# A two-layer encoder trunk on one core: the FFN's norm factor moved behind gate and up, one set of weight pools for all stages, and the last hidden pair kept on chip

## Chip, core and metric

One core of a Trainium2 chip runs one program. The metric is its device time in microseconds (us), the median of the runs shown. TensorE (PE) multiplies; VectorE (DVE), ScalarE (ACT) and GpSimd (POOL) work elementwise; SyncE (SP) issues every DMA of this program, in order.

## What is computed

A residual stream h of 1024 tokens by 1024 features goes through two layers in float32. Layer 0 mixes tokens with differential attention, layer 1 with neighbourhood attention. Cut to what matters here:

```
for i in range(DEPTH):                                    # DEPTH = 2
    h = h + mixer_i(rmsnorm(h, norm_mix[i]))              # attention, then @ w_o
    h = h + swiglu(rmsnorm(h, norm_ffn[i]), w_gate, w_up, w_down)
    gate = sigmoid(rmsnorm(h, norm_ple[i]) @ ple_w_gate[i])
    h = h + gate * (p[i] @ ple_w_proj[i])
return rmsnorm(h, norm_final)

def rmsnorm(x, g):  return x * rsqrt(mean(x*x) + eps) * g
def swiglu(h, wg, wu, wd):  return (silu(h @ wg) * (h @ wu)) @ wd    # hidden width 2816
```

## The kernel before

Activations lie feature-major: a tile holds 128 features by 1024 tokens (two halves of 512). Every float32 operand is split into a high and a low part (`split`, L99: ACT or POOL writes the high part, DVE subtracts it from the source for the low part), and a product is three matmul passes, high by high, high by low and low by high (`PASSES`).

The stages of a layer, in the order of the program:

- **Mixer**, `diff_attention` (L300) or `neighborhood_attention` (L438), with `qk` (L231) and `v_units` (L287) for its projections, both by L219 or L294 on the normed input `hnT`. Eight pairs of heads leave split outputs `ot`; seven go to DRAM (`keep`, L548), the last stays on chip. `out_proj_first` (L554) multiplies the first `EARLY = 6` pairs by w_o, adds the residual and stores the sum in DRAM (`hp`); its matmuls (L572) fill the gaps of the last attention unit.
- **Out projection**, `out_proj` (L578): the remaining two pairs (L597), added to `hp` (L599); per half of the tokens `norm_blocks` (L147) then computes the norm (`norm`, L114: ACT squares, DVE sums them, PE sums over partitions at L126, a POOL power, DVE writes diagonals at L132, PE broadcasts them at L134, and DVE multiplies each of the 8 feature tiles at L137).
- **Gate and up**, `gate_up` (L604): both matrices are multiplied by a 2x2 block scheme with seven products instead of eight (`seven`, L209; order 0, 5, 4, 1, 6, 3, 2). Its moving operands are seven tiles `bt` (16 KB a partition each), sums and differences of the four blocks of the normed activations that `norm_blocks` makes with DVE and POOL. Its stationary operands are seven such sums of the weights: `prepare` loads two raw tiles, `blocks` (L180) makes four sums on POOL (L190) and splits seven results on ACT and DVE. There are 11 pairs of 256 hidden features, a group for gate and a group for up in each, and a group is 7 products of 12 matmuls (84) into four PSUM banks. `after` (L641) adds the products, applies silu (L637) or multiplies by the gate (L639). `hand_over` (L664) makes seven blocks of the pair's result (POOL L673, then `split`) and writes them to DRAM (`ad`, L671).
- **Down**, `down` (L693): five chunks of pairs (2, 2, 2, 2, 3); per chunk the blocks `b` come back from DRAM (L706, a ring of 22 tiles), and four output pairs `dp` of seven products each run at L719, with weights through `blocks` again. DVE and POOL add into h at L725; h itself is loaded from DRAM (`hd`, L821).
- **Input embedding**, `ple` (L747): p @ w_proj at L762 from operands loaded before `down`, a norm, 16 blocks of the gate product (L219), then the next norm.

Buffers come from pools on a stack, and a new tile's first write waits for the last reader of what lay at that place. `stage` (raw weights), `slab` (split weights) and `t4` (work tiles) are opened and closed with the stages (`pools`, L86; `build`, L785). What an engine does in which order is set by a scheduler that walks a modelled timeline, so it isn't the order of the code; each engine, SP included, then takes its own list strictly in order.

Of the kernel before, what the change touches and what calls it, by code (L numbers as in the profile page):

```python
# [12 lines left out]
F32 = mybir.dt.float32  # L13
# [18 lines left out]
CHUNKS = ((0, 1), (2, 3), (4, 5), (6, 7), (8, 9, 10))  # L32

# [15 lines left out]
EARLY = 6  # L49
# [5 lines left out]
class Trunk:  # L55
    def __init__(self, ctx, tc, a):
# [5 lines left out]
        self.stage = self.slab = self.t4 = self.ob = None  # L62
# [5 lines left out]
        self.mhalf = self.const.tile([P, 4], F32, name="mhalf")  # L68
# [17 lines left out]
    def pools(self, st, name, **bufs):  # L86
        for k, n in bufs.items():
            setattr(self, k, st.enter_context(self.tc.tile_pool(name=f"{k}_{name}", bufs=n, reuse_waits="tile")))
# [25 lines left out]
    def norm(self, h, c, i, pool, sink, order=range(KT), keep=None):  # L114
# [20 lines left out]
        for k in order:  # L135
            n = keep[:, k] if keep is not None else pool.tile([P, HALF], F32, tag="n", name="n", bufs=4)
# [10 lines left out]
    def norm_blocks(self, h, half, i, pool, bt):  # L147
        nc = self.nc
        c = slice(half * HALF, (half + 1) * HALF)

        def put(b, k, x):
            self.split((bt[b][:, 0, k], bt[b][:, 1, k]), x, nc.scalar)

        if half == 0:
            self.n0 = pool.tile([P, KT, HALF], F32, tag="n0", name="n0", bufs=1)
            self.norm(h, c, i, pool, lambda k, n: put(k // 4, k % 4, n), keep=self.n0)
            return
        n0, held = self.n0, {}

        def sink(k, n):  # L160
            if k < 4:
                held[k] = n
                return
            k -= 4
            n11, n21, n12, n22 = n0[:, k], n0[:, k + 4], held.pop(k), n
            put(2, k, n22)
            nc.gpsimd.tensor_tensor(out=n11, in0=n12, in1=n11, op=ALU.subtract)
            put(4, k, n11)
            nc.gpsimd.tensor_tensor(out=n12, in0=n22, in1=n12, op=ALU.subtract)
            put(6, k, n12)  # L170
            t2 = pool.tile([P, HALF], F32, tag="t2", name="t2", bufs=2)
            nc.vector.tensor_tensor(out=t2, in0=n22, in1=n11, op=ALU.subtract)
            put(5, k, t2)
            nc.gpsimd.tensor_tensor(out=n21, in0=n21, in1=t2, op=ALU.subtract)
            put(3, k, n21)

        self.norm(h, c, i, pool, sink, order=(0, 4, 1, 5, 2, 6, 3, 7))


    def blocks(self, a11, a12, a21, a22, pool, tag, shape, bufs):  # L180
        nc = self.nc
        out = [None] * 7

        def put(b, x):
            w = pool.tile([P, 2] + shape, F32R, tag=tag, name="w", bufs=bufs)
            self.split((w[:, 0], w[:, 1]), x, nc.scalar)
            out[b] = w

        def sub(o, x, y, op=ALU.subtract):
            nc.gpsimd.tensor_tensor(out=o, in0=x, in1=y, op=op)  # L190

        put(0, a11)
        s1 = pool.tile([P] + shape, F32, tag="s1", name="s1", bufs=1)
        s2 = pool.tile([P] + shape, F32, tag="s2", name="s2", bufs=1)
# [36 lines left out]
    def qk(self, u, pools, bias=None, q_scale=1.0):  # L231
        nc = self.nc
        qkp, psd = pools["qk"], pools["d"]
# [4 lines left out]
        for which in range(2):  # L238
            w = self.weights(pools["wqk"][2 * u + which], self.slab, "slab")
            b = None if bias is None else bias[:, which * 8 + u:which * 8 + u + 1]  # L240
            for half in range(2):
# [27 lines left out]
                else:  # L269
# [4 lines left out]
                    for x in (kh, kl):  # L274
                        for m, (to, src) in enumerate(((bot, top), (top, bot))):
                            nc.gpsimd.tensor_scalar(out=x[to, m, c], in0=x[src, m, c].bitcast(F32), scalar1=1.0,
                                                    scalar2=0.0, op0=ALU.mult, op1=ALU.add)
        return qs, kh, kl
# [8 lines left out]
    def v_units(self, pair2, wv, psd, sink, ws=None):  # L287
        ws = ws or [self.weights(wv[2 * pair2 + s], self.slab, "slab") for s in range(2)]
        for t in range(NT):
            ps = psd.tile([P, 256], F32, tag="d", name="d")  # L290
# [9 lines left out]
    def diff_attention(self, first):  # L300
        nc, tc, a = self.nc, self.tc, self.a
        with ExitStack() as st:
            pool = lambda name, bufs, **k: st.enter_context(tc.tile_pool(name=name, bufs=bufs, reuse_waits="tile", **k))
            pools = {"qk": pool("da_qk", 1), "wqk": a["da_qk"]}
            vp = pool("da_v", 1)
# [132 lines left out]
    def neighborhood_attention(self):  # L438
        nc, tc, a = self.nc, self.tc, self.a
        with ExitStack() as st:  # L440
            pool = lambda name, bufs, **k: st.enter_context(tc.tile_pool(name=name, bufs=bufs, reuse_waits="tile", **k))
            pools = {"qk": pool("na_qk", 1), "wqk": a["na_qk"]}
            vp = pool("na_v", 1)
# [11 lines left out]
            def values(p4, psd):  # L455
# [8 lines left out]
                self.v_units(p4, a["na_v"], psd, sink)  # L464
# [72 lines left out]
            values(0, psd)  # L537
            ops = self.qk(0, pools, bq)
# [39 lines left out]
    def out_proj(self, layer, wo, h, ps, np, op, bt):  # L578
# [8 lines left out]
        ws = []  # L587
        for dt in range(KT):
            ws.append(self.weights(wo[dt, :, EARLY * P:], op, f"w{dt}", cols=late * P))
            nc.sync.dma_start(out=h[dt], in_=self.hp[dt])  # L590
        for half in range(2):
            c = slice(half * HALF, (half + 1) * HALF)
            for dt in range(KT):
                acc = ps.tile([P, HALF], F32, tag="mm", name="mm")
                for k in range(late):
                    for n, (i, j) in enumerate(PASSES):
# [313 lines left out]
```

## Time and profile before

| | us |
|---|---|
| median of 3 runs | 3023.63 (3020.64 to 3026.23) |
| the profiled execution | 3023.98 |
| its span, first to last instruction | 3022.2 |
| PE busy | 2739.8 (91%) |
| DVE, POOL, ACT busy | 2130.2, 1325.6, 1217.8 |
| mean granted TensorE clock | 0.956 |

The page of the profile gives busy shares and 40 slices of the span. Idle time of PE is best read from its list of waits and from its timeline, and the load of the other engines from a table by stage, since a share over the whole span mixes stages with different limits.

### The profile page before, as it was taken

Reading aid. Unit: us, or ns where it says so; the run is one execution under the profiler, and the core shown is the slowest. Engines: PE = TensorE matmul, PEld = TensorE weight load, DVE = VectorE, ACT = ScalarE, POOL = GpSimd, SP = SyncE. Lnnn points to the kernel's source line nnn. Section 1 sums busy time; section 2 is a strip of 40 time slices with the busy share of each in tenths; the row PEclk is TensorE's granted clock in tenths of the full one; section 3 lists DMA queues with packets and bytes.
Section 4 is the critical chain, followed back from the end, with each engine's and each line's share of the span. In section 5 each row is a group of like instructions: output and inputs, shape, how many; then the busy total and the mean of one; then the engine's idle time right before and its main releaser. Section 6 shows DMA issues by size and latency. Waiting matters only on the chain. (4 is left out here: it accounts for less than half of the span.)

```text
span 3022.2 us, 38402 instructions
## 1 busy us (share of the span) xinstructions
PE 2739.8 (91%) x13272; PEld 2255.1 (75%) x13272; DVE 2130.2 (70%) x3947; ACT 1217.8 (40%) x2534; POOL 1325.6 (44%) x1240
## 2 busy tenths in 40 slices
PE   6999999997599999599997999999399999789998
PEld 5787888885477878478786888888287788567876
DVE  6798878776767666498584666765866667568766
ACT  4454546443444443233332544542344344323241
POOL 1344443431555555477221443432255555457621
PEclk8999999998799999799998999999699999989999
DMA  3001010324244443866132112144333444486312
GB/s 114 28 29 42 29 42 27 147 100 160 63 153 141 145 154 133 313 258 251 35 119 82 54 69 75 47 170 163 117 116 143 153 153 153 159 330 252 138 63 105
DMA packets 106321, 379.59 MB, mean 126 GB/s; under 512 B 12176, under 2 KB 14352, under 8 KB 102032
## 3 DMA queue, kind: packets, MB, share of 16 engines
q1 hardware_dynamic: 106128, 377.15, 34.5%
q8 instruction: 105, 1.72, 0.2%
q14 instruction: 88, 0.72, 0.1%
HBM read 256.52 MB, written 120.59 MB: 125 GB/s over the span
## 5 line engine op out<-in xcount | busy, mean ns | idle before, releaser
L631 PE MATMUL mm<-bt,w 128*128 128x512 f32 x3696 | 870.4, 397 | 62.6 <-ACT w L101 59.6
L631 PEld LDWEIGHTS mm<-bt,w 128*128 128x128 f32 x3696 | 695.2, 189 | 240.2 <-ACT w L101 62.7
L719 PE MATMUL mm<-b,w 128*128 128x512 f32 x1848 | 432.8, 395 | 72.0 <-DMA b<-ad 63.2
L719 PEld LDWEIGHTS mm<-b,w 128*128 128x128 f32 x1848 | 348.1, 190 | 156.8 <-issue 65.2
L104 DVE TENSOR_TENSOR w<-raw,w 128x512 fp32r<-128x512 f32 (+2 forms) x420 | 356.2, 865 | 50.8 <-ACT w L101 50.4
L219 PE MATMUL d<-hnT,w 128*128 128x512 f32 x1536 | 386.3, 399 | 0.0
L219 PEld LDWEIGHTS d<-hnT,w 128*128 128x128 f32 x1536 | 287.0, 189 | 64.3
L101 ACT CAST w<-raw 128x512 fp32r<-128x512 f32 (+2 forms) x420 | 210.6, 527 | 213.0 <-POOL raw L190 109.2
L103 POOL TENSOR_SCALAR w<-st 128x1024 fp32r<-128x1024 f32 (+2 forms) x120 | 134.3, 1121 | 335.5 <-PE mm L219 100.9
L294 PE MATMUL d<-w,hnT 128*128 128x256 f32 x1536 | 227.2, 294 | 16.0 <-POOL w L103 7.7
L294 PEld LDWEIGHTS d<-w,hnT 128*128 128x128 f32 x1536 | 210.5, 198 | 27.7 <-POOL w L103 9.3
L725 POOL TENSOR_TENSOR h<-h,u 128x512 f32<-128x512 f32 x120 | 169.4, 1426 | 119.0 <-DVE u L725 118.4
L104 DVE TENSOR_TENSOR w<-s,w 128x512 fp32r<-128x512 f32 (+2 forms) x168 | 123.4, 749 | 126.4 <-ACT w L101 126.4
L190 POOL TENSOR_TENSOR s<-raw 128x512 f32<-128x512 f32 (+2 forms) x84 | 95.3, 1134 | 267.2 <-DMA raw<-gu 221.0
L366 ACT ACTIVATE e<-e,mx 128x1024 f32<-128x1024 f32 x128 | 147.3, 1151 | 124.7 <-DVE mx L364 113.4
L104 DVE TENSOR_TENSOR w<-st,w 128x1024 fp32r<-128x1024 f32 (+2 forms) x120 | 136.7, 1141 | 82.4 <-POOL w L103 81.4
L219 PE MATMUL mm<-hnT,w 128*128 128x512 f32 x768 | 188.5, 406 | 4.8 <-ACT hnT L101 3.2
L219 PEld LDWEIGHTS mm<-hnT,w 128*128 128x128 f32 x768 | 147.1, 193 | 45.4 <-issue 7.4
L101 ACT CAST at<-tr 128x512 fp32r<-128x512 f32 (+2 forms) x288 | 132.0, 481 | 106.2 <-PE tr L515 67.5
L281 PE MATMUL s<-kh,qs 128*128 128x512 f32 (+2 forms) x384 | 153.4, 409 | 23.2 <-DVE mx L358 12.6
L104 DVE TENSOR_TENSOR at<-tr,at 128x512 fp32r<-128x512 f32 (+2 forms) x288 | 155.7, 550 | 22.5 <-ACT at L101 16.7
L381 POOL TENSOR_SCALAR e<-e,rc 128x1024 f32<-128x1024 f32 x64 | 74.2, 1160 | 217.3 <-DVE rc L379 212.1
(144 smaller groups left out, 4608.1 us busy)
## 6 DMA issues: line engine op xcount, KB each, us to landing
ad<-put SPq DMA_DIRECT2D x154, 512.0 KB, 2.8
b<-ad SPq DMA_DIRECT2D x154, 512.0 KB, 8.4
raw<-gu SPq DMA_DIRECT2D x88, 512.0 KB, 4.8
raw<-wd SPq DMA_DIRECT2D x32, 512.0 KB, 7.3
st<-wpg SPq DMA_DIRECT2D x32, 512.0 KB, 3.6
ot<-ot SPq DMA_DIRECT2D x14, 1024.0 KB, 3.9
o<-ot SPq DMA_DIRECT2D x14, 1024.0 KB, 7.9
st<-da_qk SPq DMA_DIRECT2D x16, 512.0 KB, 3.4
```

Of the source, the lines that this page charges most:

```text
L101: hi_engine.copy(out=w[0], in_=src)
L103: hi_engine.tensor_scalar(out=w[0], in0=src, scalar1=1.0, scalar2=0.0, op0=ALU.mult, op1=ALU.add)
L104: self.nc.vector.tensor_tensor(out=w[1], in0=src, in1=w[0].bitcast(F32), op=ALU.subtract)
L190: nc.gpsimd.tensor_tensor(out=o, in0=x, in1=y, op=op)
L219: self.nc.tensor.matmul(ps, w[:, i, kt * P:(kt + 1) * P], self.hnT[half][:, j, kt, :], start=kt == 0 and n == 0, stop=kt == KT - 1 and n == 2)
L281: self.nc.tensor.matmul(s, qs[:, m, qc], (kh, kl)[part][:, m, kc], start=part == 0, stop=part == 1)
L294: self.nc.tensor.matmul(ps, self.hnT[t // 4][:, i, k, c], ws[k // 4][:, j, (k % 4) * 256:(k % 4 + 1) * 256], start=k == 0 and n == 0, stop ...
L366: nc.scalar.activation(out=e[m], in_=e[m], func=AF.Exp, bias=mx[:, m:m + 1], scale=SLOPES[h], accum_out=sm[:, m:m + 1])
L381: nc.gpsimd.tensor_scalar(out=e[0], in0=e[0], scalar1=rc[:, 0:1], scalar2=0.0, op0=ALU.mult, op1=ALU.add)
L631: nc.tensor.matmul(acc, w[b][:, i, k * P:(k + 1) * P], bt[b][:, j, k], start=first and k == 0 and n == 0, stop=k == 3 and n == 2, skip_gro ...
L719: nc.tensor.matmul(acc, w[b][:, i, q], mv[b, q][:, j], start=first and q == 0 and m == 0, stop=q == n - 1 and m == 2, skip_group_check=True)
L725: eng.tensor_tensor(out=o, in0=x, in1=y, op=ALU.add)
```

## The change

- **Norm.** `norm_blocks` goes. `out_proj` takes tiles dt and dt + 4 together, multiplies x by the norm's gain alone (ACT), makes the seven `bt` of these two tiles at once (`moving_blocks`) and collects squares (ACT into one `sq` buffer, POOL adds). The factor 1/rms is computed once for all 1024 tokens (`inverse_rms`), issued inside the first gate group after product 5, and kept as `rb`. In `use` the gate's product is multiplied by `rb` before silu, and by `rb` again after it, which brings up's factor.
- **Pools.** One `stage` (2), `slab` (3) and `t4` (4) live as long as the kernel. `packed` puts the seven weight results into slabs (2 to a slab in gate and up, 4 in a two-pair chunk of down) over three shared slabs and two of the stage's own.
- **Down.** The last pair's seven blocks stay on chip (`kept`); the ring has 18 tiles, and the loads of the first chunk and `kept` lie where `bt` was. A three-pair weight tile comes as two loads.
- **Input embedding.** Its operands are loaded and split after `down` (`ple_proj`), through the ring's tiles.
- **Smaller.** `EARLY` is 5, so the late out projection has 3 pairs. Layer 1 computes the first half of its values and half of its first q before it needs the second half of the normed tokens (`lead`). Pools of odd and even head units stand apart.

```diff
-EARLY = 6
+EARLY = 5
+RING_B = 18
...
+        self.pools(ctx, stage=2, slab=3, t4=4)
...
+    def moving_blocks(self, n, k, pool, bt):
...
+        put(0, n11)
+        sub(t3, n22, n12, nc.gpsimd)
+        sub(n12, n12, n11)
+        sub(t2, n22, n12)
+        put(5, t2)
+        put(4, n12)
+        put(1, n21)
+        put(6, t3)
+        sub(n21, n21, t2, nc.gpsimd)
+        put(3, n21)
+        put(2, n22)
+    def inverse_rms(self, acc, diag, rb):
...
+        for b in range(NT):
+            nc.tensor.matmul(ps[:, 0, b:b + 1], acc[:, b * P:(b + 1) * P], self.mean, start=True, stop=True)
...
+        nc.gpsimd.tensor_tensor(out=rs, in0=rs, in1=self.mhalf, op=ALU.pow)
+        for half in range(2):
+            for b in range(4):
+                nc.vector.tensor_scalar(out=diag[:, half, b], in0=self.ident, scalar1=rs[:, 4 * half + b:4 * half + b + 1],
+                                        scalar2=None, op0=ALU.mult)
+            bc = self.ps_tr.tile([P, 4, P], F32, tag="tr", name="bc")
+            nc.tensor.matmul(bc, self.ones1, diag[:, half], start=True, stop=True)
+            nc.scalar.copy(out=rb[:, half * HALF:(half + 1) * HALF], in_=bc.rearrange("p a b -> p (a b)"))
+    def packed(self, slabs):
+        state = [None, 0, 0]
+        def place(n):
+            if state[0] is None or state[1] + 2 * n > 2 * D:
+                pool, tag = slabs[state[2] % len(slabs)]
+                state[:] = [pool.tile([P, 2 * D], F32R, tag=tag, name="w"), 0, state[2] + 1]
...
     def out_proj
+        for k in range(KT // 2):
+            for dt in (k, k + KT // 2):
+                w = self.weights(wo[dt, :, EARLY * P:], op, "w", cols=late * P, bufs=2)
...
+                    nc.vector.tensor_tensor(out=x[:, c], in0=ac, in1=x[:, c], op=ALU.add)
+                    nc.scalar.activation(out=g[:, c], in_=x[:, c], func=AF.Copy,
+                                         scale=self.g[:, 3 * layer + 1, dt:dt + 1])
+                nc.sync.dma_start(out=self.hd[dt], in_=x)
+            self.moving_blocks(n, k, op, bt)
...
+                    sq = op.tile([P, HALF], F32, tag="sq", name="sq", bufs=1)
+                    nc.scalar.activation(out=sq, in_=x[:, c], func=AF.Square)
+                    nc.gpsimd.tensor_tensor(out=acc[:, c], in0=acc[:, c], in1=sq, op=ALU.add)
...
     def gate_up
                 def use(f, c, src, eng):
                     if which == 0:
-                        nc.scalar.activation(out=gt[:, f, c], in_=src, func=AF.Silu)
+                        eng.tensor_tensor(out=o, in0=src, in1=rb[:, c], op=ALU.mult)
+                        nc.scalar.activation(out=o, in_=o, func=AF.Silu)
+                        nc.gpsimd.tensor_tensor(out=o, in0=o, in1=rb[:, c], op=ALU.mult)
...
                     elif b == 5:
-                        add(out=t["u2"], in0=acc, in1=t["p1"], op=ALU.add)
+                        add(out=t["u2"], in0=ac, in1=t["p1"], op=ALU.add)
+                        if pr == 0 and which == 0:
+                            with tc.issue_after(self.end.ins):
+                                self.inverse_rms(acc, op, rb)
...
+            bp.release()
+            bp = tc.alloc_tile_pool(name=f"db{layer}", bufs=1, side="right", reuse_waits="tile")
+            ring = [self.ring_load(bp, pr, b) for b in ORDER for pr in CHUNKS[0]]
+            kept = {b: bp.tile([P, 2, HALF], F32R, tag=f"k{b}", name="kept") for b in range(7)}
+            hand_over(PAIRS_F - 1, kept.get)
...
     def build
-                    pt = [self.weights(a["pT"][layer, k], pw, f"pt{k}") for k in range(2)]
-                    wpp = [self.weights(a["wpp"][layer, k], pw, f"wp{k}") for k in range(2)]
-                    self.down(layer, h, ps)
+                self.down(layer, h, ps, bp, ring, kept)
+                proj = self.ple_proj(layer, ps, bp, pool("pj"))
```

The order of instructions moves at three places that the prediction speaks of.

SP's list at the start of layer 0's `down`, before (`b` are the blocks that `down` reads back, `put` those that `hand_over` writes, `raw` weights, `h` the residual stream):

```order
L821 DMA h_10849<-hd 128x1024
L710 DMA raw<-wd 128x1024
L671 DMA ad<-put 128x1024
L710 DMA raw<-wd 128x1024
L671 DMA ad<-put 128x1024 x3
L710 DMA raw<-wd 128x1024
L108 DMA st<-pT 128x1024
L706 DMA b<-ad 128x1024 x12
L108 DMA st<-pT 128x1024
L706 DMA b<-ad 128x1024 x9
```

The same place now:

```order
L754 DMA ad<-put 128x1024 x6
L810 DMA raw<-wd 128x1024 x3
L787 DMA b<-ad 128x1024 x18
L937 DMA h_10797<-hd 128x1024
L937 DMA h_10798<-hd 128x1024
L937 DMA h_10799<-hd 128x1024
```

The eight loads of h stood ahead of the blocks and now stand behind 18 of them; three weight loads stand ahead of both. The same rows with the semaphores that they wait for:

```order
L810 DMA raw_10978<-wd 128x1024 [waits DMAHW3_49,DMAHW1_49,DVE_49]
L787 DMA b_10735<-ad_95 128x1024 [waits DMAHW4_49,PE_49]
L787 DMA b_10737<-ad_95 128x1024 [waits DMAHW5_49,PE_49]
L787 DMA b_10739<-ad_95 128x1024 [waits DMAHW6_49]
L787 DMA b_10741<-ad_95 128x1024 [waits DMAHW7_49]
```

Only the first two loads of blocks wait for PE. By the semaphore's values in the built program the first waits for product 0 of the last group and the second for product 3, the sixth of seven (it lies where `bt` 3 was), and the third weight load waits for the DVE split that frees the first one's stage buffer; the rest stand behind them.

PE's list where layer 0 goes from the out projection into gate and up, before (`bt` numbers: 7088 is block 0, 7093 block 5, 7092 block 4):

```order
L597 MATMUL mm<-o,w 128x512 x3
L597 MATMUL mm<-ot,w 128x512 x3
L126 MATMUL sums<-mean,acc 128x1 x4
L134 MATMUL bc<-diag,ones_73 128x512
L126 MATMUL sums<-mean,acc 128x1 x4
L134 MATMUL bc<-diag,ones_73 128x512
L631 MATMUL mm<-bt_7088,w 128x512 x12
```

Now (7039 is block 0, 7040 block 5, 7042 block 1, 7043 block 6, 7044 block 3, 7045 block 2):

```order
L707 MATMUL mm<-bt_7042,w 128x512 x2
L707 MATMUL mm<-bt_7044,w 128x512 x6
L179 MATMUL sums<-mean,acc 128x1 x4
L707 MATMUL mm<-bt_7043,w 128x512 x12
L179 MATMUL sums<-mean,acc 128x1 x4
L188 MATMUL bc<-diag,ones_82 128x512 x2
L707 MATMUL mm<-bt_7045,w 128x512 x12
L707 MATMUL mm<-bt_7039,w 128x512 x12
L707 MATMUL mm<-bt_7042,w 128x512 x12
L707 MATMUL mm<-bt_7040,w 128x512 x2
```

Both sums and both broadcasts stood between the out projection and the first product; now one pair of broadcasts stands late in the first group.

PE's list from layer 0's last gate block to layer 1's first values, before:

```order
L219 MATMUL mm<-hnT_12897,w 128x512 x120
L126 MATMUL sums<-mean,acc 128x1 x4
L134 MATMUL bc<-diag,ones_73 128x512
L294 MATMUL d<-w,hnT_12896 128x256 x96
L294 MATMUL d<-w,hnT_12897 128x256 x96
```

Now (`hnT_12899` is the first half of the tokens, `hnT_12900` the second):

```order
L261 MATMUL mm<-hnT_12900,w 128x512 x122
L348 MATMUL d<-w,hnT_12899 128x256 x48
L128 MATMUL sums<-mean,acc 128x1 x4
L348 MATMUL d<-w,hnT_12899 128x256 x39
L136 MATMUL bc<-diag,ones_82 128x512
L348 MATMUL d<-w,hnT_12899 128x256 x9
L261 MATMUL d<-hnT_12899,w 128x512 x24
L348 MATMUL d<-w,hnT_12900 128x256 x96
```

The norm of the second half stood alone ahead of layer 1's values; now 96 value matmuls and 24 of q stand around it.

## Rows read from the trace of the kernel before

**Rows 1.** The page: busy time by engine, the 40 slices of PE and its granted clock.

```profile
PE 2739.8 (91%) x13272; PEld 2255.1 (75%) x13272; DVE 2130.2 (70%) x3947; ACT 1217.8 (40%) x2534; POOL 1325.6 (44%) x1240
...
PE   6999999997599999599997999999399999789998
...
PEclk8999999998799999799998999999699999989999
```

**Rows 2.** Waits of PE, longest first: us in total, times, longest.

```profile
PE mm L719 <- DMA b<-ad: 63.2, 14, 29.7
PE mm L631 <- ACT w L101: 59.6, 2, 29.8
PE sums L126 <- DVE acc L123: 48.1, 5, 14.4
```

**Rows 3.** Table by stage: stretch, length, busy us (instructions), clock, DMA share, GB/s.

```profile
756.00:786.00 30.00, 0.42 (x1) 0.42 (x2) 30.00 (x31) 12.53 (x21) 18.57 (x12) 0.50 0.11 35
786.00:1222.00 436.00, 434.70 (x1848) 347.16 (x1847) 290.38 (x347) 177.75 (x315) 230.79 (x161) 0.99 0.40 137
1222.00:1252.00 30.00, 0.47 (x1) 0.50 (x2) 12.61 (x20) 6.44 (x16) 15.08 (x16) 0.54 0.89 335
```

**Rows 4.** Table by stage again, over two entries into gate and up and one into down.

```profile
711.10:828.10 117.00, 66.00 (x268) 51.38 (x269) 88.49 (x121) 46.40 (x78) 45.01 (x32) 0.77 0.30 104
1222.00:1276.80 54.80, 22.98 (x85) 16.38 (x86) 26.71 (x41) 11.06 (x27) 23.66 (x24) 0.72 0.95 369
2106.30:2231.00 124.70, 75.32 (x311) 59.22 (x310) 88.66 (x121) 46.46 (x78) 43.97 (x31) 0.78 0.33 115
```

**Rows 5.** Timeline of layer 0's entry: start, us, engine, line, tiles, count, idle before.

```profile
711.10 0.42 DVE L104 TENSOR_TENSOR ot<-o,ot 128x256 fp32r<-128x256 f32 x1 [0.47 <-ACT ot L101]
...
741.73 4.29 DVE L104 TENSOR_TENSOR bt<-n,bt 128x512 fp32r<-128x512 f32 x7
...
749.57 1.83 PE L126 MATMUL sums<-mean,acc 128*128 128x1 f32 x8 [14.37 <-DVE acc L123]
...
753.75 2.04 PE L134 MATMUL bc<-diag,ones 128*128 128x512 f32 x2 [2.34 <-DVE diag L132]
```

**Rows 6.** Groups by line and shape in gate and up, 830 to 1200: busy, mean ns.

```profile
L673 POOL TENSOR_TENSOR t<-gt 128x512 f32<-128x512 f32 x20 | 33.5, 1675 | 24.9 <-DVE gt L639 24.9
L190 POOL TENSOR_TENSOR s<-s,raw 128x512 f32<-128x512 f32 x18 | 23.3, 1295 | 0.7
L104 DVE TENSOR_TENSOR put<-gt,put 128x512 fp32r<-128x512 f32 x49 | 54.6, 1129 | 1.1
L646 DVE TENSOR_TENSOR u<-mm,p 128x512 f32<-128x512 f32 x19 | 12.9, 680 | 0.0
```

**Rows 7.** Timeline of DVE and POOL in gate and up, 1030 to 1040.

```profile
1030.31 2.38 DVE L104 TENSOR_TENSOR put<-gt,put 128x512 fp32r<-128x512 f32 x2
1030.53 1.61 POOL L673 TENSOR_TENSOR t<-gt 128x512 f32<-128x512 f32 x1 [2.49 <-DVE gt L639]
...
1037.93 1.62 POOL L673 TENSOR_TENSOR gt<-gt,t 128x512 f32<-128x512 f32 x1
1038.54 1.56 DVE L104 TENSOR_TENSOR put<-t,put 128x512 fp32r<-128x512 f32 x1
```

**Rows 8.** Timeline of SP at the entry into down: blocks read back.

```profile
1257.80 10.56 SPq L706 DMA_DIRECT2D b<-ad  x9
```

**Rows 9.** Loads of the embedding's gate weights: time to landing.

```profile
DMA to landing us min/median/max: 3.3/3.6/5.2
```

**Rows 10.** Timeline of PE at the end of layer 0.

```profile
1589.80 8.33 PE L219 MATMUL mm<-hnT,w 128*128 128x512 f32 x35
1602.48 1.21 PE L126 MATMUL sums<-mean,acc 128*128 128x1 f32 x8 [4.36 <-DVE acc L123]
...
1616.63 0.79 PE L294 MATMUL d<-w,hnT 128*128 128x256 f32 x2 [7.73 <-POOL w L103]
1620.30 5.90 PE L294 MATMUL d<-w,hnT 128*128 128x256 f32 x35 [2.87 <-DVE w L104]
```

More of the change, by code (lines that the diff above doesn't have):

```diff
@@ L134, in norm @@
         nc.tensor.matmul(bc[:, :nb], self.ones1, diag[:, :nb], start=True, stop=True)
-        for k in order:
-            n = keep[:, k] if keep is not None else pool.tile([P, HALF], F32, tag="n", name="n", bufs=4)
+        for k in range(KT):
+            n = pool.tile([P, HALF], F32, tag="n", name="n", bufs=4)
             nc.vector.scalar_tensor_tensor(out=n[:, :w], in0=h(k, c), scalar=self.g[:, i, k:k + 1],
@@ L144, in norm_t, with put @@
         self.norm(h, c, i, pool, lambda k, n: self.split((dst[:, 0, k, o], dst[:, 1, k, o]), n, self.nc.scalar))
[L147 removed]
+    def moving_blocks(self, n, k, pool, bt):
         nc = self.nc
[L149 to L151 removed]
+        n11, n12, n21, n22 = n[0][:, :HALF], n[0][:, HALF:], n[1][:, :HALF], n[1][:, HALF:]
+        def put(b, x):
             self.split((bt[b][:, 0, k], bt[b][:, 1, k]), x, nc.scalar)
[L154 to L177, printed above, removed]
@@ L192, in blocks, with sub @@
+        def sub(os, xs, ys, op=ALU.subtract):
+            for o, x, y in zip(os, xs, ys):
+                nc.gpsimd.tensor_tensor(out=o, in0=x, in1=y, op=op)
+        a11, a12, a21, a22 = zip(*parts)
+        s1, s2, o = [], [], 0
+        for x, n in zip(a11, widths):
+            for j, l in enumerate((s1, s2)):
+                v = sums[:, j, o:o + n]
+                l.append(v.rearrange("p (q c) -> p q c", c=x.shape[2]) if len(x.shape) == 3 else v)
+            o += n
         put(0, a11)
-        s1 = pool.tile([P] + shape, F32, tag="s1", name="s1", bufs=1)
@@ L586, in out_proj @@
         os.append(self.last.rearrange("p l b q -> p l (b q)"))
[L587 to L596, printed above, removed]
-                        nc.tensor.matmul(acc, ws[dt][:, i, k * P:(k + 1) * P], os[k][:, j, c],
-                                         start=k == 0 and n == 0, stop=k == late - 1 and n == 2)
-                nc.vector.tensor_tensor(out=h[dt][:, c], in0=acc, in1=h[dt][:, c], op=ALU.add)
-                nc.sync.dma_start(out=self.hd[dt, :, c], in_=h[dt][:, c])
-            self.norm_blocks(lambda k, c: h[k][:, c], half, 3 * layer + 1, np, bt)
+        acc = op.tile([P, S], F32, tag="acc", name="acc")
@@ L785, in build @@
+                if not last:
+                    nc.sync.dma_start(out=self.hs[dt, :, c], in_=h[dt][:, c])
+            if last:
+                self.norm(hv, c, 3 * layer + 3, np,
+                          lambda k, n: nc.sync.dma_start(out=a["out"][k, :, c], in_=n))
+            else:
+                self.norm_t(hv, c, 3 * layer + 3, np)
     def build(self):
@@ new lines, in build @@
+                if layer == 0:
+                    first = []
+                    with tc.tile_pool(name="x", bufs=1, reuse_waits="tile") as xp:
+                        for q in range(4):
+                            xt = xp.tile([P, KT, 256], F32, tag="x", name="xt", bufs=4)
+                            nc.sync.dma_start(out=xt, in_=a["xq"][q])
+                            if q in (1, 2):
+                                first.append(self.weights(a["da_v"][q - 1], self.slab, "slab"))
+                            self.norm_t(lambda k, c, xt=xt: xt[:, k], slice(q * 256, (q + 1) * 256), 0, xp)
+                    self.diff_attention(first)
+                else:
+                    self.neighborhood_attention()
```

314 lines of the change are left out of this document (185 added, 129 removed).

## The prediction

> **What bounds the kernel now.** I read the page first, then PE's waits, the tables by stage, and the timeline of the places with low busy shares. The page shows PE busy for 91% of the span, with dips in the slices and a lower granted clock in the same slices [rows 1]. So PE is the bound where it runs, and what can be won lies in the dips: 3022.2 less 2739.8 is 282 us. PE's waits name them: the two longest are the entries into gate and up (L631 waits for a weight split, 29.8 us at most, and L126 for the norm's sum, 14.4), and the entries into down (L719 waits for blocks, 29.7) [rows 2]. The tables by stage show what limits each. In the first entry DVE is busy for all of 30 us and POOL for 18.57, PE for 0.42. Gate and up proper is PE alone: 434.70 of 436 us, or 434.70 / 1848 = 0.235 us a matmul, DVE at 290.38. In the down entry the DMA engines are full (0.89) [rows 3]. These two sorts of entry cost 117.0, 124.7 and, for down's first, 54.8 us [rows 4].
>
> Two durations carry most of the sum. A DVE split with both inputs in SBUF takes 4.29 / 7 = 0.61 us where POOL is idle [rows 5]. A POOL tensor_tensor on 512 columns takes 1.295 us in the weight sums, 1.675 in hand_over; the DVE splits beside it go up to 1.129, while L646, which reads PSUM, stays at 0.680 [rows 6]. So DVE operations on SBUF and POOL's stretch each other. How much: in 756 to 786, the 31 DVE instructions are 24 with two SBUF inputs and 7 that read PSUM, and 24 x 0.61 + 12 x 1.29 = 30.1 of 30.00 us: nothing overlapped [rows 3]. In 1030.31 to 1040.10, five POOL operations (5 x 1.29) and seven such DVE operations (7 x 0.61) are 10.7 us of work in 9.79, a ratio of 0.91 [rows 7]. These are my two bounds for work that the change adds there.
>
> The sum is made against the profiled execution, 3023.98; the median is 3023.63, the same but for 0.35.
>
> **A, the entry into gate and up.** Removed: the norm ahead of the blocks, with its wait of 14.37 for the last sum, then 2.34, and the 29.8 after it [rows 2, 5]. In their place the out projection makes the blocks tile by tile and PE multiplies as they come. By the order of the changed kernel, from the split that ends the attention to the last block DVE has 48 operations on SBUF (48 x 0.61 = 29.3) and POOL 28 (22 by 1.29 = 28.4, and six weight roundings of 384 columns at half that, an estimate, 3.9). Taken one after another, as in 756 to 786, that is 61.6, and 4.4 until the first product is there: 66. Then POOL still has four additions of squares (5.2) before the sums, the power, diagonals and broadcast (1.83 + 2.34 + 2.04 as before, 6.2 [rows 5]): 77.4. PE's remaining 36 matmuls of the first group (8.4), a wait of some 3 for a weight of the second group, since POOL multiplies by `rb` before it makes that weight's sums, and 60 of the second group (14.1) give 102.9 until the end of the second group. `EARLY = 5` puts 48 matmuls (11.3 us) into this stretch, where PE waits anyway; out of layer 0's tail it takes 33, worth 0 to 33 x 0.235 = 7.8, taken at half, 3.9. So layer 0 gains 117.0 + 3.9 - 102.9 = 18.0 and layer 1 124.7 - 102.9 = 21.8 [rows 4]: **-40**. Ends: at a ratio of 0.91 the 61.6 become 56, -51; if layer 0's and 1's first blocks come late by the waits for `t4` buffers that x now shares with the weight sums, 10 in each, -20.
>
> **B, the entry into down.** Counted from the start of up's last group (19.7 us of PE, 84 x 0.235), PE has work until 19.7. SP's list decides: the third weight load waits for a split at about 16, the second load of blocks for product 3 (72 matmuls, 16.9), the other 16 behind it. One load of 512 KB follows another every (10.56 - 0.32) / 8 = 1.28 us in such a burst [rows 8]; the first lands some 3.6 after it is issued, by the loads that stand alone [rows 9]. So block 12 lands at 19.8 + 12 x 1.28 = 35.2, block 18 at 42.8 and the first of h at 44.1. The DVE addition with h frees the PSUM bank that the second output pair wants: PE goes on at about 44.9, with the 42 matmuls of the first pair and two more (44, 10.3 us) done meanwhile, a loss of 44.9 - 19.7 - 10.3 = 15, and 3 for additions piled up. Before it was 54.8, of which 85 matmuls are 85 x 0.235 = 20.0: a loss of 35 [rows 4]. **-17 in each layer, -34.** Ends: with blocks landing before product 3 is over, -40; with h at the end of a slower queue and PE waiting all the way, as now, -6.
>
> **C, layer 0 to layer 1.** PE waits 4.36, does the sums, and waits on to 7.73 and 2.87: from 1589.80 + 8.33 = 1598.1 to 1620.3 are 22.2 us with little in them [rows 10]. Now 96 half-width value matmuls and 24 of q need only the first half, and cover it: 96 x 5.90 / 35 = 16.2 [rows 10] and 24 x 0.235 = 5.6. Left is a first weight's split, so **-17**, between -21 and -8.
>
> **D, gate and up.** Added per pair: 8 multiplications by `rb`, five on POOL and three on DVE, one of those from PSUM. POOL has 20 operations of 1.29 a pair instead of 15, DVE 25 on two SBUF inputs. One after another that is 25.8 + 25 x 0.61 = 41.1, against PE's 168 x 0.235 = 39.5 a pair: +1.6 in each of 22 pairs, +35. By the ratio 0.91 it is 37.4 and hidden behind PE: 0. The longer stretch of alternation speaks for the second, the exclusive 30 us for the first, and I take the middle: **+18**.
>
> The Trainium skill, "SBUF — State Buffer", section on the two separate sides, says that DVE and GpSimd share a port pair under a lock held for a whole instruction, the loser blocked; it speaks against putting more POOL work here. The trace agrees in that L646, which reads PSUM, keeps its 0.680 us [rows 6], and differs in the 0.91 [rows 7]. By the rule D would be +35 and the total 2970.
>
> **E, smaller.** The embedding's operands are now loaded and split after down: 8 loads and 8 splits, of which the first can stand on the path (3.6 to land [rows 9], half of it covered): **+2**, 0 to 6. The weight loads of a three-pair chunk are twice as many, of half the size, on an engine that has room in 786 to 1222 (DMA share 0.40 [rows 3]): 0, the cover being the 63 matmuls, 14.8 us, that PE does with each of these tiles. The `kept` pair saves seven stores and loads of 512 KB a layer; they were beside other work outside the entry: 0.
>
> Sum: -40 - 34 - 17 + 18 + 2 = -71, so 3024 - 71 = **2953 us**.
>
> **Rivals.** (1) Gate and up stays with PE and the entries come out at their good ends: -51 - 40 - 20 + 0 + 0 = -111, 2913; from 2895 on. The ratio in rows 7 speaks for it, the full DVE of rows 3 against. (2) Down's entry gains nothing, since SP takes its list in order and h stands behind 18 blocks: the stall by blocks becomes a stall by h. Then B is 0 and the sum -37, 2987, up to 3010 with D at 35. For it speaks that the DMA engines are full there already (0.89 [rows 3]); against, that seven blocks of the last pair don't travel. (3) The side that is slower: gate and up becomes DVE's. DVE must do, per pair, 25 operations on SBUF and 10 from PSUM (10 x 0.68 = 6.8); it exceeds PE's 39.5 when an SBUF operation takes over 32.7 / 25 = 1.31 on average. Splits are now at 1.129 beside POOL [rows 6]; POOL's busy share there goes from 230.79 / 436 = 0.53 [rows 3] by 20 / 15 to 0.71. The stretch over 0.61 being 0.52 at a share of 0.53, it is 0.70 at 0.71: 1.31, just at the point. At 1.56, a stretch such as the longest split of rows 7 shows, a pair takes 45.8: 22 x 6.3 = +139 in place of +18, and the sum is +50: 3074. At 1.47 gains and losses are even. It needs every operation to be stretched as the longest is. (4) The change does not do what it says: PE's sums stand inside the first group but bind it (product 4 of 7 waits for the last square), A is then half, -20, 2973; inside the range.
>
> **Numbers.** Forecast with D between 0 and 35, 2920 to 2985: 0.5. Rival 1, below 2920: 0.2. Rivals 2 and 4 with D at its end, 2985 to 3018: 0.16, which makes 0.86 for faster. Rival 3 and what else makes it slower by over 0.2%: 0.1. Within 0.2%, 6 us, about what a measurement of this kernel tells from no change: 0.04. The range, 2895 to 3000, leaves out some 0.04 below and 0.16 above (rival 3, no change, and the upper part of rival 2).
>
> **What would show it.** PE in the first entry: no wait over 15 us, L707 products ahead of the sums, second gate group's end 103 after the last `ot` split (A). Down's first chunk: a wait of PE named by h or by DVE's addition of some 15 us, not 29 (B). From layer 0's last L261 matmul to the first value matmul under 5 us (C). In gate and up, PE busy nearly 99% (rival 1), or waiting for DVE or POOL some 1 us a pair (D), 5 or more (rival 3); the mean of DVE's splits there tells which. It is wrong above all if D's stretching is on another scale than rows 6 and 7, or if h comes later than 44 us after up's last group begins.

## The result and the profile after

The changed kernel takes **3095.03 us** (median of 4 runs, 3093.92 to 3096.33) against 3024.93 of the kernel before (4 runs): a ratio of 1.0233, 95% interval 1.0215 to 1.0251. It is slower by 70 us where 71 us less were forecast, and outside the range. Its profiled execution is 3095.93, the span 3094.1.

Time between the last matmuls of the stages, read from the traces (the stage's first matmul where the row says so). *Own tiles* and *last version* are experiments below.

| us | before | after | own tiles (e1) | last version (e11) |
|---|---|---|---|---|
| start to the end of layer 0's second group of gate and up | 827.9 | 826.4 | 826.5 | 812.7 |
| the other 20 groups (10 pairs), layers 0 and 1 | 394.1, 394.7 | 413.5, 412.8 | 412.5, 413.2 | 393.6, 393.6 |
| to down's first matmul | 29.5, 29.7 | 3.4, 3.6 | 3.9, 3.4 | 3.4, 3.6 |
| down, first to last matmul | 222.1, 223.5 | 271.8, 272.4 | 229.3, 230.1 | 232.0, 230.7 |
| to the first gate matmul of the embedding | 27.6, 28.5 | 40.3, 39.2 | 37.0, 36.9 | 36.0, 35.1 |
| the embedding's gate matmuls | 96.9, 97.0 | 97.2, 97.4 | 98.0, 97.4 | 97.3, 97.9 |
| to the end of layer 1's first q (96 matmuls) | 69.3 | 50.2 | 50.2 | 64.2 |
| to the end of layer 1's second group | 563.4 | 547.5 | 545.0 | 543.5 |
| to the end | 17.9 | 18.5 | 18.0 | 18.8 |

So the stalls that the change was to remove are gone, and down itself, gate and up, and the way from down to the embedding are longer by more. PE's waits over the whole span of the changed kernel (us in total, times, longest):

```profile
PE sums L128 <- DVE acc L125: 39.0, 5, 11.3
PE mm L822 <- ACT w L103: 30.3, 20, 3.6
PE mm L707 <- ACT t L723: 29.4, 20, 3.1
PE mm L822 <- ACT t L831: 27.8, 18, 3.6
...
PE mm L822 <- DMA b<-ad: 11.9, 14, 3.6
```

The waits of 29.7, 29.8 and 14.4 of [rows 2] have no counterpart (the 11.3 in the first line is PE's wait for the first sum at the kernel's start, as before); in their place stand many of up to 3.6 us, in down (L822) and once a pair in gate and up (L707, which waits for ScalarE's copy of a group's first product into `p1`). The table by stage, in the columns of [rows 3]; the first and second line are layer 0's and layer 1's down, the third is layer 0's gate and up from near the end of its first group on:

```profile
1243.00:1515.00 272.00, 237.16 (x924) 179.15 (x924) 184.34 (x286) 67.21 (x183) 153.95 (x158) 0.95 0.50 189
2666.00:2939.00 273.00, 236.64 (x925) 178.51 (x925) 183.02 (x286) 67.31 (x183) 153.81 (x157) 0.96 0.51 189
799.00:1240.00 441.00, 424.89 (x1776) 337.53 (x1776) 354.10 (x375) 177.74 (x316) 330.37 (x215) 0.99 0.37 135
```

In down no engine is full: PE 87%, DVE 68%, POOL 57%, the DMA engines 0.50. That looks like a chain of waits and not like a full engine. In gate and up DVE and POOL are now at 80% and 75%; POOL stood at 53% [rows 3].

### The profile page after: what moved, and what is told of

Its sections match the earlier page's. It is cut to its first block, busy times and chain, and to the rows that moved or that the text cites. A ratio compares the mean times of both kernels' runs of the same rounds, so it can differ in the third digit from the quotient of the medians.

```text
span 3094.1 us, 38448 instructions
## 1 busy us (share of the span) xinstructions
PE 2820.4 (91%) x13272; PEld 2281.7 (74%) x13272; DVE 2277.1 (74%) x4023; ACT 1250.2 (40%) x2626; POOL 1572.7 (51%) x1408
## 5 line engine op out<-in xcount | busy, mean ns | idle before, releaser
L707 PE MATMUL mm<-bt,w 128*128 128x512 f32 x3696 | 895.2, 404 | 51.0 <-ACT t L723 29.4
L707 PEld LDWEIGHTS mm<-bt,w 128*128 128x128 f32 x3696 | 707.3, 192 | 239.5 <-ACT t L723 38.5
L822 PE MATMUL mm<-b,w 128*128 128x512 f32 x1680 | 440.1, 416 | 76.8 <-ACT w L103 29.9
L106 DVE TENSOR_TENSOR w<-raw,w 128x512 fp32r<-128x512 f32 (+2 forms) x460 | 379.6, 845 | 129.3 <-ACT w L103 128.2
L822 PEld LDWEIGHTS mm<-b,w 128*128 128x128 f32 x1680 | 326.0, 198 | 184.9 <-ACT w L103 42.0
L105 POOL TENSOR_SCALAR w<-st 128x1024 fp32r<-128x1024 f32 (+3 forms) x128 | 146.5, 1146 | 360.3 <-PE mm L261 66.4
L828 POOL TENSOR_TENSOR h<-h,t 128x512 f32<-128x512 f32 x120 | 161.4, 1359 | 229.1 <-DVE t L828 196.3
L106 DVE TENSOR_TENSOR w<-s,w 128x512 fp32r<-128x512 f32 (+2 forms) x184 | 194.8, 1064 | 26.4 <-ACT w L103 23.2
L106 DVE TENSOR_TENSOR w<-st,w 128x1024 fp32r<-128x1024 f32 (+3 forms) x128 | 142.6, 1118 | 91.6 <-POOL w L105 91.4
L567 POOL TENSOR_SCALAR e<-e,sm 128x384 f32<-128x384 f32 (+1 forms) x128 | 75.3, 590 | 184.3 <-DVE sm L566 158.3
```

The lines of the kernel that those rows point to most:

```text
L105: hi_engine.tensor_scalar(out=w[0], in0=src, scalar1=1.0, scalar2=0.0, op0=ALU.mult, op1=ALU.add)
L106: self.nc.vector.tensor_tensor(out=w[1], in0=src, in1=w[0].bitcast(F32), op=ALU.subtract)
L567: nc.gpsimd.tensor_scalar(out=e[:, :n], in0=e[:, :n], scalar1=sm, scalar2=0.0, op0=ALU.mult, op1=ALU.add)
L707: self.end = nc.tensor.matmul(acc, w[b][:, i, k * P:(k + 1) * P], bt[b][:, j, k], start=first and k == 0 and n == 0, stop=k == 3 and n == ...
L822: nc.tensor.matmul(acc, w[b][:, i, q * P:(q + 1) * P], mv[b, q][:, j], start=first and q == 0 and m == 0, stop=q == n - 1 and m == 2, skip ...
L828: eng.tensor_tensor(out=o, in0=x, in1=y, op=ALU.add)
```

## The experiments

Theories: **T**, down's weights come late because the sums of a weight tile share four tiles with p1, u2 and u3; **S**, because of two raw buffers; **R**, because weight loads stand behind blocks on SP; **P**, DVE and POOL stretch each other; **Q**, gate and up loses by the latency ahead of ScalarE's copy; **N**, the embedding's norm comes late because of the place of its tiles; **V**, the start does because of the place of layer 0's values. What points to T in the trace: of POOL's list in down, these rows hold the additions of a pair and the weight sums of a coming one.

```profile
1331.88 1.29 POOL L828 TENSOR_TENSOR h<-h,t 128x512 f32<-128x512 f32 x1 [3.15 <-DVE t L828]
1333.13 0.74 POOL L227 TENSOR_TENSOR s<-raw 128x256 f32<-128x256 f32 x1
...
1335.32 2.69 POOL L828 TENSOR_TENSOR h<-h,t 128x512 f32<-128x512 f32 x2
1337.96 0.91 POOL L227 TENSOR_TENSOR raw<-raw,s 128x256 f32<-128x256 f32 x1
1345.92 1.28 POOL L828 TENSOR_TENSOR h<-h,t 128x512 f32<-128x512 f32 x1 [7.04 <-DVE t L828]
1347.16 0.74 POOL L227 TENSOR_TENSOR s<-raw 128x256 f32<-128x256 f32 x1
1348.43 2.51 POOL L828 TENSOR_TENSOR h<-h,t 128x512 f32<-128x512 f32 x2 [0.54 <-DVE t L828]
1350.90 0.91 POOL L227 TENSOR_TENSOR s<-s,raw 128x256 f32<-128x256 f32 x1
```

PE then starts again at 1352.30 after a wait for ACT's split of that second sum (`s<-s,raw`):

```profile
1351.84 0.41 ACT L103 CAST w<-s 128x256 fp32r<-128x256 f32 x1 [1.70 <-POOL s L227]
1352.30 10.00 PE L822 MATMUL mm<-b,w 128*128 128x512 f32 x35 [1.87 <-ACT w L103]
```

In the built program `s_11169<-raw` waits for POOL's `h6<-h6,t_11006`, the last addition of two pairs earlier: an output pair takes three of the four tiles in turn (sums, p1 with u2, u3), so the sums of pair m lie where u3 of pair m - 2 lay, and the scheduler puts them on POOL's list behind additions that wait for PE. In these rows it is the place in the list that holds the sum: the last addition of two pairs earlier is over by 1338.0, and POOL later stands idle for 7.04 us ahead of an addition that waits for DVE, with the sum behind it.

**e1, own work tiles.** The edit:

```diff
-                    a2, b2 = (self.t4.tile([P, 2, HALF], F32, tag="t4", name="t") for _ in range(2))
-                    t = {"p1": a2[:, 0], "u2": a2[:, 1], "u3": b2[:, 0]}
+                    t = {k: tp.tile([P, HALF], F32, tag=k, name=k, bufs=2) for k in ("p1", "u2", "u3")}
```

> Down's p1, u2 and u3 get six tiles of their own (12 KB a partition more); the four shared tiles are left to the weight sums. In the changed kernel down's 924 matmuls take 271.8 and 272.4 us in the two layers, 222.1 and 223.5 before. Theory T (the sum of a weight tile waits for a shared work tile, so weights come late): down returns to within 10 us of before in each layer, time 3000 to 3020. Theory S (weights come late because their raw loads wait for one of two stage buffers): under 8 us a layer, 3080 to 3095. Theory R (SP's list: blocks that wait for a ring tile hold the weight loads): under 8 us a layer. Theory P (DVE and POOL stretch each other): no change, 3095.

Measured: 3001.82 us, 0.9928 of before (0.9913 to 0.9943). Down takes 229.3 and 230.1 us. POOL's waits for DVE's additions in layer 0's down, which held the weight sums up, fall; the first fence is the changed kernel, the second e1, the third e1's row of the table by stage:

```profile
POOL h L828 <- DVE t L828: 95.7, 26, 8.2
```

```profile
POOL h L828 <- DVE u L828: 33.5, 19, 4.4
```

```profile
1242.90:1472.20 229.30, 221.72 (x925) 173.93 (x926) 184.27 (x289) 65.49 (x180) 156.55 (x157) 0.99 0.60 227
```

PE's mean clock there is 0.99 again. T holds; S, R and P can't be the cause by themselves, since raw buffers, SP's ring and the number of operations are as in the changed kernel. Whether more tiles under the same sharing would do as well was not tried.

**e2, three raw buffers; e3, own work tiles and two raw buffers.** The edit of e2 (e3: both, with `bufs=2`):

```diff
-                        raw = self.stage.tile([P, D], F32, tag="st", name="raw")
+                        raw = rp.tile([P, D], F32, tag="raw", name="raw", bufs=3)
```

> Down's raw weights get three buffers of their own in place of the two shared stage buffers. Theory S: down loses 30 us or more in each layer, time 3010 to 3035. Theory T: under 10 us a layer, 3080 to 3095. Theories R and P: under 10 us a layer; by R the loads are issued no earlier, since they stand behind loads of blocks.

> Both of the former in part: own work tiles, and two raw buffers of down's own, so that the embedding's operands have the stage buffers free. Theory T: as with own work tiles alone, 3000 to 3020 less some 5 to 15 us for the embedding's loads and the norm behind them, if these wait for the stage. Theory S with T in series: only this one recovers the whole, 2995 to 3010, and each alone recovers under half. Theory R or P: over 3070.

Measured: e2 3110.85 us (3099.6 to 3117.2; its profiled run is the shortest), e3 3026.43, neither in a range that its theories gave. Down takes 266.3 and 267.9 in e2, 226.1 and 226.9 in e3: buffers for raw weights are worth 3 to 6 us a layer, and S falls. Both lose 15 to 18 us at each entry into down (3.4 becomes 21.8 in e2), which no theory expected. SP's timeline of e2 shows it: the first weight loads now stand behind 16 loads of blocks, of which this row holds 15.

```profile
1235.18 12.96 SPq L787 DMA_DIRECT2D b<-ad  x15
1249.15 2.82 SPq L811 DMA_DIRECT2D raw<-wd  x3
```

PE waits 21.83 us there, for the split of such a weight. The shared stage buffers were free earlier, and their loads stood ahead of the blocks. The expected 5 to 15 us for the embedding's loads didn't show either (27.6 before, 37.3 in e3).

**e12, the kernel before with shared tiles.** The opposite: before, with only that sharing put in.

```diff
-            tp = st.enter_context(tc.tile_pool(name=f"dt{layer}", bufs=1, reuse_waits="tile"))
+            tp = st.enter_context(tc.tile_pool(name=f"dt{layer}", bufs=4, reuse_waits="tile"))
...
-                    t = {k: tp.tile([P, HALF], F32, tag=k, name=k, bufs=2) for k in ("p1", "u2", "u3")}
+                    a2, b2 = (tp.tile([P, 2, HALF], F32, tag="t4", name="t") for _ in range(2))
+                    t = {"p1": a2[:, 0], "u2": a2[:, 1], "u3": b2[:, 0]}
...
-        s1 = pool.tile([P] + shape, F32, tag="s1", name="s1", bufs=1)
-        s2 = pool.tile([P] + shape, F32, tag="s2", name="s2", bufs=1)
+            s = sums.tile([P, 2, HALF], F32, tag="t4", name="s")
```

> The kernel before, with one edit: in down the sums of a weight tile and p1, u2 and u3 share four tiles, as in the changed kernel. Ring, raw buffers, slabs and the order of loads stay. Theory T: down grows from 222.1 and 223.5 us to 255 to 275 a layer, time 3090 to 3125. Rival (the sharing does harm only with the changed kernel's raw buffers and ring): under 10 us a layer, 3023 to 3044.

Measured: 3176.83 us, 1.0494 of before (1.0477 to 1.0512). Down takes 298.3 and 298.5 us. Its row of the table by stage, and PE's wait there:

```profile
1253.40:1551.70 298.30, 246.58 (x926) 192.15 (x927) 153.39 (x254) 60.90 (x156) 141.44 (x139) 0.89 0.47 175
```

```profile
PE mm L724 <- ACT w L101: 46.2, 17, 5.5
```

So the sharing is enough by itself, and costs more here than expected: the changed kernel has room for 20 weight blocks where this has 12, which may soften it (not tried). With the waits the mean granted clock falls too, to 0.89, so PE is busy for longer with the same matmuls.

**e4, late silu; e5, no second factor.** The edits:

```diff
+                        while late:
+                            with tc.issue_after(self.cp.ins):
+                                late.pop()()
...
-                            use(0, f2, t["u2"], nc.vector)
+                            late.append(lambda: use(0, f2, t["u2"], nc.vector))
```

```diff
-                        nc.gpsimd.tensor_tensor(out=o, in0=o, in1=rb[:, c], op=ALU.mult)
```

> The gate's last piece (second half, product 2) is multiplied by the factor, put through silu and multiplied again only after ScalarE's copy of the next group's first product; nothing is left out. In the changed kernel PE waits for that copy (L723) 29.4 us in all, 20 times, once a pair. Theory Q (the copy queues on ScalarE behind a silu, which now waits for a DVE multiplication): the wait goes, gate and up falls by 12 to 18 us a layer (441 to some 425), time 3060 to 3072. Theory P (POOL and DVE are too busy in gate and up, 5 POOL and 3 DVE operations more a pair): the wait moves elsewhere, under 5 us a layer, 3085 to 3095.

> On top of own work tiles (3001.8): the second multiplication by the factor (POOL, four operations a pair) is left out, so up's factor is missing from the output. Gate and up took 412.5 and 413.2 us for its last 20 groups there, 394.1 and 394.7 before the change. Theory P (POOL and DVE, the operations added for the factor, stretch each other): it falls by 12 to 18 us a layer, time 2966 to 2978. Theory Q (only the latency of the first multiplication ahead of silu and of ScalarE's copy counts): it falls by under 5, time 2992 to 3002.

Measured: e4 (on the changed kernel) 3088.93 us, with 409.1 and 409.6 us for the 20 groups; e5 (on e1) 2963.28 us, with 394.1 and 394.7, the numbers of before to a tenth and a little more than P's 12 to 18 us (18.4 and 18.5). PE's waits in 830 to 1200, for the changed kernel, e4 and e5:

```profile
PE mm L707 <- ACT t L723: 12.4, 8, 3.1
```

```profile
PE mm L707 <- DVE t L725: 10.6, 9, 1.4
PE mm L707 <- ACT t L723: 0.9, 2, 0.6
```

```profile
PE mm L707 <- ACT t L722: 0.2, 1, 0.2
```

The copy is where PE sees the lateness, not its cause: when the silu no longer stands ahead of the copy, DVE is late by nearly as much. Four POOL operations a pair fewer take back the whole of it. P holds. The changed kernel's groups in that stretch (columns of [rows 6]) show the stretching on both sides, against the same weight sum and split of the kernel before in the second fence:

```profile
L716 POOL TENSOR_TENSOR gt<-gt,rb 128x512 f32<-128x512 f32 x36 | 53.5, 1505 | 10.1 <-ACT gt L715 10.1
L106 DVE TENSOR_TENSOR w<-s,w 128x512 fp32r<-128x512 f32 x36 | 51.9, 1442 | 6.0 <-ACT w L103 4.9
L227 POOL TENSOR_TENSOR s<-raw 128x512 f32<-128x512 f32 x18 | 31.4, 1742 | 0.0
L725 DVE TENSOR_TENSOR t<-mm,t 128x512 f32<-128x512 f32 x18 | 12.2, 677 | 0.0
```

```profile
L104 DVE TENSOR_TENSOR w<-s,w 128x512 fp32r<-128x512 f32 x37 | 32.9, 890 | 42.2 <-ACT w L101 42.2
L190 POOL TENSOR_TENSOR s<-raw 128x512 f32<-128x512 f32 x18 | 23.7, 1317 | 98.9 <-DMA raw<-gu 98.9
```

POOL's weight sum went from 1.317 to 1.742 us, DVE's split of it from 0.890 to 1.442; the DVE addition that reads PSUM stayed at 0.68 [rows 6].

**e6, the norm's place; e7, EARLY 6.** In e6 `acc` and `sq` of the embedding's norm come from a pool below `pj`, and the ring has 17 tiles; e7 is one number.

```diff
-RING_B = 18
+RING_B = 17
...
-        acc = pool.tile([P, HALF], F32, tag="acc", name="acc", bufs=2)
+        acc = qp.tile([P, HALF], F32, tag="acc", name="acc", bufs=2)
...
+                qp = pool("nq")
                 proj = self.ple_proj(layer, ps, bp, pool("pj"))
```

> On top of own work tiles: the squares and sums of the input embedding's norm get a pool of their own below the others (8 KB; for it the ring has 17 tiles, not 18), so that they don't lie where the ring's tiles hold the embedding's operands. Theory N (the squares stand on ScalarE behind 16 copies of p @ w_proj because their place comes free only with its last matmul): PE's wait of 7 to 8 us for the norm's sum goes, the stretch from down's end to the first gate matmul falls from 37 to 28 us a layer, time 2982 to 2988. Rival (the splits of the embedding's operands on DVE delay the norm): under 3 us a layer, 2996 to 3004.

> On top of own work tiles: EARLY is 6 again, so 48 matmuls (11.3 us of PE) a layer go from the late out projection back to the fillers of the last attention unit. The prediction held that moving them out of the tail gains (3.9 us in layer 0): then this is slower by 2 to 12 us in all, 3004 to 3014. Rival (the tail had gaps for them, and the late out projection, which waits for its weights' splits, is longer for the third pair): faster by 5 to 20, 2982 to 2997.

Measured: e6 2998.73 us. The way from down to the embedding's gate is 30.5 and 28.2 us (37.0 and 36.9 in e1), as N says, but layer 0's end gave 9 back (the stretch to layer 1's first q is 59.4 for 50.2), so the whole stayed above N's 2982 to 2988. Why the norm was late is seen on ACT. In e1 the first square of the norm stands behind the last of 16 copies:

```profile
1494.04 0.59 ACT L880 COPY pj<-mm 128x512 f32<-128x512 f32 x1 [0.77 <-PE mm L878]
1494.52 0.63 ACT L123 ACTIVATE acc<-h 128x512 f32<-128x512 f32 x1
```

In e6 squares run ahead of and among the copies, as they did before the change; this one stands 19 us ahead of e1's first:

```profile
1475.40 0.63 ACT L124 ACTIVATE sq<-h 128x512 f32<-128x512 f32 x1 [0.24 <-DVE acc L126]
```

e7 took 3008.94 us: `EARLY = 5` is worth 7, as its expectation has it.

**e8, the factor after down.** h is multiplied by the factor's reciprocal when it is loaded and by the factor after the last chunk:

```diff
-                        nc.gpsimd.tensor_tensor(out=o, in0=o, in1=rb[:, c], op=ALU.mult)
...
+            nc.vector.reciprocal(out=ib, in_=rb)
+            for dt in (0, 4, 1, 5, 2, 6, 3, 7):
+                (nc.vector if dt < 4 else nc.gpsimd).tensor_tensor(out=h[dt], in0=h[dt], in1=ib, op=ALU.mult)
```

> On top of own work tiles: up's factor is put on after down (it is one number a token): h is multiplied by its reciprocal when it is loaded and by the factor after the last chunk, 8 and 16 operations a layer in place of 44 on POOL in gate and up; nothing is left out. Theory P: gate and up as with the second factor left out, less 3 to 6 us a layer for what stands at the ends of down, time 2972 to 2988. Theory Q: slower by 2 to 10 us, 3004 to 3012.

Measured: 3014.31 us. Gate and up falls to 393.6 in both layers, as P says, and down gives it back (243.6 and 245.7 us), and 13.6 more go at layer 0's end. Both theories missed the sum.

**e9 to e11, towards a better version.** e9 gives layer 0's attention one pool for its units again:

```diff
-            odd, vp, even = pool("da_qk1", 1), pool("da_v", 1), pool("da_qk0", 1)
-            pools["qk"] = even, odd
+            both, vp = pool("da_qk", 1), pool("da_v", 1)
+            pools["qk"] = both, both
```

> On top of own work tiles: layer 0's attention has one pool for its head units again, with the values above it, as before the change (layer 1 keeps them apart). Theory V (with the units apart, the tile of values lies where the input tiles of the first norm lay, so the splits of values wait until 61 us and PE with them): PE's first score matmul comes 8 to 12 us earlier (98.4 to some 88), time 2989 to 2995. Rival (the start waits for the norm's chain anyway, or the attention tail gives it back): under 3 us, 2999 to 3004.

Measured: 2991.56 us, 10 below e1; PE's first score matmul comes at 90.0 for 98.4. In the changed kernel ACT's first splits of values, and PE's matmuls behind them, wait until 61 us; in e9 they run from 26.8:

```profile
61.01 1.48 ACT L103 CAST v<-d 128x128 fp32r<-128x128 f32 x8
62.45 7.81 PE L348 MATMUL d<-w,hnT 128*128 128x256 f32 x47 [7.78 <-DVE v L106]
```

```profile
26.82 0.43 ACT L103 CAST v<-d 128x128 fp32r<-128x128 f32 x2 [1.24 <-PE d L348]
```

e10 keeps h out of down's sums, on top of e9 (ring of 17); e11 adds the norm's own place (ring of 16).

```diff
+                        def fin(dt, c, eng=nc.vector):
+                            if xs:
+                                o = h[dt][:, c]
+                                eng.tensor_tensor(out=o, in0=o, in1=rb[:, c], op=ALU.mult)
+                                add(o, o, xs[dt][:, c], eng)
```

> On top of the former: down sums its chunks without h, and its first chunk writes where it added; after the last chunk the sum is multiplied by the factor and h, loaded then, is added. So POOL's 44 second multiplications in gate and up go, and 8 loads of h leave the entry (ring of 17 tiles, two tiles for h). Theory P: gate and up 394 us for its last 20 groups; down's entry shorter by some 5 a layer since DVE's first additions no longer wait for h; 2 to 5 back at down's end: time 2940 to 2960. Rival (additions at down's end delay the norm by as much as gate and up gains): 2975 to 2995.

> On top of the former: the squares and sums of the embedding's norm in a pool of their own (ring of 16 tiles). Theory N: 5 to 9 us a layer less between down's end and the first gate matmul, 10 to 16 us under the former. Rival (what it gives there is taken again where layer 0 ends, as with a place of its own before, 9 us): 4 to 8 us under the former.

Measured: e10 2973.14 us, e11 **2960.61** us, 0.9783 of before (0.9768 to 0.9797): faster than both kernels. In e10 gate and up is at 393.6, but down is no shorter (229.9), so a gain from DVE's first additions doesn't show, and e10 lies outside the times of both its theories; layer 0's end costs 14 us as in e8:

```profile
PE d L348 <- DVE v L106: 11.2, 1, 11.2
```

The splits of layer 1's first values stand on DVE's list behind the norm's multiplications there. What in the scheduler's model puts them there in e6, e8, e10 and e11, and not in e1, stays open. From e10 to e11 the total falls by 12.5 us, in N's range; the way to the embedding's gate gives 4.5 and 4.0 of it, less than N's 5 to 9 a layer.

## Why the prediction was wrong, point by point

- **The step that failed** is a term that the sum doesn't have: down after its entry is put at nothing, as if the change left it as it was, and the sharing of the four `t4` tiles was priced only at layer entry, in term A's lower end (10 us each). It cost 42 us a layer in down (271.8 and 272.4 against 229.3 and 230.1), shown from both sides by e1 and e12; that the place on POOL's list is the way it works is read from rows, not tested apart. The sign of the result hangs on it: without it the same kernel is faster than before by 0.7%. From -71 to the +72 of the two profiled spans are 143 us: 80 lie in down and its entry, 23 in A, 21 in E, 20 in D, and C takes 2 off.
- **B**, the entry into down: -34 forecast. With own tiles the entry and down together give 251.6 to 233.2 and 253.2 to 233.5, **-38**. The form was another than worked out, and that the sum comes near is partly luck: PE waits at the entry for 3.4 us, not 15, which gains 26 a layer, and down, which was to stay, takes 7 more a layer even with own tiles.
- **C**, layer 0 to 1: -17 forecast, 69.3 to 50.2 is **-19**. Right.
- **D**, gate and up: +18 was taken from the middle of 0 and 35; measured **+37.5** (19.4 and 18.1) in 20 of the 22 pairs. The choice of the middle failed, and the exclusive end had the right size: 20 POOL operations of 1.29 and 25 DVE operations of 0.61 one after another are 41.1 us a pair, and e1 takes 412.5 / 10 = 41.3. That they agree to 1% doesn't show that nothing overlaps. In 830 to 1200 of the changed kernel the trace has 182 POOL operations and 224 DVE operations on SBUF, 371.4 us one after another; one or both sorts run in 345.4 us, and neither runs in 24.6. While they run the ratio is 345.4 / 371.4 = 0.93, close to the 0.91 of [rows 7]. So that ratio was fair, and what failed is the step from it to "hidden behind PE", which leaves no room for gaps in which neither of the two runs. The Trainium skill, "SBUF — State Buffer", section on the two separate sides, states an exclusive lock between DVE and GpSimd; the +35 worked out by it was the better number, while the trace shows an exclusion that isn't whole (0.93).
- **A**, the entry into gate and up: -40 forecast. Up to the second group layer 0 gained 1.5 and layer 1 (from its first q) 15.9. The mechanism holds (`bt` is done 63 us after the last `ot` split, at 779.6 from 716.1; forecast 61.6), though the second group ends 110.3 us after that split, not 102.9; and layer 0 came to the split 5 us late (711.1 before). The step behind that had no price at all: the pools of odd and even units put the values where the first norm's input tiles lay, and e9 takes 14 us off this stretch (826.5 to 812.4) and 10 off the whole.
- **E**, the embedding: +2 forecast, **+23.4** measured (40.3 and 39.2 for 27.6 and 28.5). The loads were priced, the place of the norm's tiles wasn't; e6 shows 6.5 and 8.7 us of it, and own tiles (e1) had taken 3.3 and 2.3 off.
- **Rivals**: 3 has the right side by the wrong mechanism. Gate and up did become bound by DVE and POOL, but at +37.5, below its break-even, and alone would have left the kernel faster. Rival 1 falls with D. Rival 2 is refuted: the entry gained. Rival 4 doesn't show either: PE's waits for the last squares (L179) are 2.1 us in both layers together.

## What to carry to other kernels

When a change merges buffer pools, count for each pool how many tiles one round of the loop takes and which reader, how many rounds ago, frees the next one: here three tiles a round out of four let a weight's sums start only after the last reader of two rounds earlier, and that sharing alone turned a gain into a loss. Do the same for places: a tile that lies where an earlier stage's tile lay starts when its last reader is done, and the stage that suffers can be far from the edit. An overlap ratio from a stretch in which two engines are full prices their work and not the gaps between: before calling added work hidden, leave room for the gaps (24.6 of 370 us here).

## What was not expected of the hardware

DVE operations on SBUF and POOL's cost a pair nearly as much as one after another (41.1 us worked out, 41.3 measured), though POOL's share is only 75% there and a part of them overlaps (0.93 of the sum while they run). And short stalls, up to 3.6 us in the changed kernel and 5.5 in e12, spread over down, cost twice: the mean granted clock was 0.95 and 0.89 there, and the same 924 matmuls kept PE busy for 237.2 and 246.6 us, against 221.7 in e1 at 0.99. It can be seen behind the wait of 1.87 us that ends at 1352.30: from 1354.0 to 1356.8 the granted clock is 0.50, the lower of its two levels (1.2 and 2.4 GHz), and matmuls start 0.43 us apart; from 1357.2 on it is 1.00, and they start 0.23 us apart.
